# Last layer's MLP for two of three token groups: the inner product in seven block products instead of eight

## The chip, the cores and the metric

The kernel runs on one core of one Trainium2 chip. The metric is the device time of one execution in microseconds. Lower is better.

A core has a matrix engine (TensorE, PE in the profile), which writes its results into eight PSUM banks, three engines for elementwise work (VectorE or DVE, ScalarE or ACT, GpSimd or POOL), and queues that issue DMAs (here mostly that of SyncE, SP).

## The reference, cut to what matters

Two layers of a decoder, 1040 prompt tokens (16 of them learned) and 8 sample tokens, all in float32. Layer 0 has a convolution module, layer 1 a recurrent one (RWKV-7), and each is followed by an MLP:

```python
h = h + out                                   # out: the mixer's, through w_o in layer 1
h = h + jnp.square(jax.nn.relu(_rmsnorm(h, norm_mlp[i]) @ w_mlp_in[i])) @ w_mlp_out[i]
...
y = _rmsnorm(h, norm_final)
```

The width is D = 1024, the hidden width of the MLP DFF = 4096. In this text the product with w_mlp_in is the inner one, the product with w_mlp_out the outer one.

## The kernel before, in words

**Layout.** Activations lie transposed: 128 features on the partitions, KT = 8 blocks of features, tokens along the free dimension. A matmul takes a 128x128 block of weights as stationary operand and up to 352 tokens as moving operand. The last layer's tokens come in three groups G2: group 0 with 328 tokens, groups 1 and 2 with 352 each.

**Precision.** A float32 product is made of three matmuls in the faster format F32R: each operand is split into a high part (a cast, on ACT) and a low part (the difference, on DVE or POOL), and `mm3` (L188) multiplies high by high, low weight by high activation, and high weight by low activation.

**Weights.** `load_raw` (L144) brings 512 KB by a DMA on SP into one of five buffers. `load_w` (L150) casts them to high parts on ACT (L158, 128x1024 at once) and makes the low parts on POOL in four operations of 128x256 (L165). Five such pairs of buffers (`open_weights`, tag w) let ACT and POOL run ahead of PE.

**The last stage** (from L1621): for group 0 the mixer's output projection (`mixer_out`, L1637: for 8 blocks m, `dense` with 24 matmuls each, then h += result on DVE and the squares for the norm), then its MLP alone, with the rest of the recurrent mixer filled in between. Then the projections of groups 1 and 2, and one MLP for both, so that each weight block serves both groups. `final` (L1662) applies the last norm, transposes and writes out.

**The MLP** (`mlp`, L322). The normalised activations are not scaled by 1/rms: `mlp_in` (L273) multiplies h by the norm's weights only, splits, and 1/rms is multiplied in when the inner result leaves PSUM (L347: max(x, 0) times 1/rms on DVE; L348: square on ACT; L141 and L142: high and low part). `inp` does one of 32 column blocks j for one group: 8 blocks k of three matmuls into one bank. `out` does the outer product: for two rows of weights (j, j+1) and each of the 8 output blocks m, six matmuls into a bank, which DVE adds to h (L360). So each pair of column blocks has 2 x 2 x 24 = 96 inner and 2 x 8 x 6 = 96 outer matmuls. There are 16 such pairs.

**What sets the order.** Inside `in_order()` PE's instructions stand in program order; the other engines' order is set by a list scheduler, which takes what is ready by its own model of time, the earliest in the program first. All engine queues are in order on the chip. `filler` spreads the steps of other work over the points of the main loop. Before, `final(0)` is spread over group 2's projection and the MLP, and group 1's `final` over the last outer products of group 2.

**PSUM**: four banks "mm" for products, one "x" for means, three "w" for transposes.

Of the kernel before, what the change touches and what calls it, by code (L numbers as in the profile page):

```python
# [8 lines left out]
F32 = mybir.dt.float32  # L9
F32R = mybir.dt.float32r  # L10
# [36 lines left out]
def hybrid_step(tc, x_prompt, x_sample, state_conv, state_shift, state_wkv, meta_tokens,  # L47
# [10 lines left out]
    with ctx:  # L58
# [129 lines left out]
        def mm3(ps, w, act, first, last):  # L188

            nc.tensor.matmul(ps, w[0], act[0], start=first, stop=False)  # L190
            nc.tensor.matmul(ps, w[1], act[0], start=False, stop=False)  # L191
            nc.tensor.matmul(ps, w[0], act[1], start=False, stop=last)  # L192
# [4 lines left out]
        def dense(w, act, n, name, fill=None):  # L197
            ps = bank(f"ps_{name}")
            for k in range(KT):
                mm3(ps[:, :n], (w[0][:, k, :], w[1][:, k, :]), [tile_of(part, k)[:, :n] for part in act], k == 0, k == KT - 1)  # L200
                if fill and k == KT // 2 - 1:
                    fill()
            return ps

# [572 lines left out]
        hsum = masks.tile([P, P], F32, name="hsum")  # L777
        nc.vector.memset(hsum, 0.0)
        for sl in HALF:
            nc.vector.memset(hsum[sl, sl], 1.0)  # L780
        cur["raw"] = pool(lm, "wrawd", 5)
        cur["mm"] = pool(lm, "psum1", 4, space=PSUM)
        cur["x"] = pool(lm, "psx1", 1, space=PSUM)
        cur["w"] = pool(lm, "psw", 3, space=PSUM)
# [7 lines left out]
        hsel = masks.tile([P, 4 * KT + 2 * (KT - 1)], F32, name="hsel")  # L792
        nc.vector.memset(hsel, 0.0)
        for q in range(2):
            for e in range(2):
                o = 2 * (KT - 1) + NH * e + q
                nc.vector.memset(hsel[HALF[q], o:o + 1], 1.0)
        head_sel = lambda p: hsel[:, 2 * (KT - 1 - p):2 * (KT - 1 - p) + 2 * NH]
# [9 lines left out]

        hspread = masks.tile([P, NH, HS], F32R, name="hspread")
        nc.vector.tensor_copy(hspread, r_head.unsqueeze(2).broadcast_to([P, NH, HS]))  # L810
# [20 lines left out]
        lorap = pool(ld, "lorap", 1)  # L831
        pr = pool(ld, "pr", 1)
# [15 lines left out]
        sps = masks.tile([P, KT, DEC], F32, name="sps")  # L848
# [772 lines left out]
        with ExitStack() as l1:  # L1621
            open_tmp(l1, N2, "2", 3, False)
            open_weights(l1, 0, {"w": 5}, "f")
# [3 lines left out]
            hidp = pool(l1, "hidp1", 2)  # L1627
            hl = {}
# [8 lines left out]
            def mixer_out(g, actp, fill, add):  # L1637
                lo, n = G2[g]
                h1 = hl[g]
                block = lambda m: load_col(rwkv_w_o[0], m, f"wo{g}_{m}", nc.gpsimd, keep=m > 0)  # L1640
# [21 lines left out]
            def final(g):  # L1662
                lo, n = G2[g]
                hv = hl[g][:, :, :n]
                accs = mean_parts(hv, n, f"f{g}", True, "facc")
# [21 lines left out]
                for j, i in enumerate(starts):  # L1687
# [3 lines left out]
                    ot = (outp if g < 2 else cur["raw"]).tile([P, D], F32, name=f"ot{g}_{i}", tag="raw")  # L1691
                    for hf in range(2):
                        pt = bank(f"pf{g}{i}{hf}", "w" if g < 2 or hf else "mm")
# [54 lines left out]
            outp = pool(l1, "outp", 1)  # L1748
# [10 lines left out]
            end = []  # L1759

            def done(g):
                end.append(filler(KT, ([final(g)], 24)))

            def fill2():
                (end[0][0] if end else fill)()
            mlp(1, [g1, group(2, actp2, hidp2, sums)], 1, nc.gpsimd, nc.vector, fill2, done)
            for it in (rest, end[0][1], final(2)):
                for _ in it:
                    pass
# [31 lines left out]
```

## Time and profile before

| | |
|---|---|
| median of 3 runs | 2635.03 us (2635.01 to 2638.54) |
| span of the profiled execution | 2635.4 us |
| PE busy | 2581.3 us, 98%, 19956 matmuls |
| DVE, ACT, POOL busy | 1707.6, 1139.1, 1457.0 us |
| projections of groups 1 and 2 | about 2054 to 2117 us |
| MLP of groups 1 and 2 | about 2117 to 2622 us |
| last `final` alone | about 2622 to 2635 us |

The span goes from the first to the last instruction of the one profiled execution; for that execution no other time is shown, so the span is the time that the sums are made against, and it lies 0.4 us above the median of the runs. A line of the profile names the line of the code, the engine, the operation, output and inputs by tile names without numbers, their shapes, and how many there are; then the busy time, the mean duration of one in ns, and the idle time of the engine ahead of them with what ended it. For PE the durations overlap: a matmul's share of the time is read from the distance of the starts, not from its duration.

### The profile page before, as it was taken

The page shows a single profiled execution, that of the slowest core. Times are in us where ns is not written, and L with a number is a line of the kernel's source. Part 1 is how long each engine was busy: PE and PEld are TensorE (multiplying, and loading weights), DVE is VectorE, ACT ScalarE, POOL GpSimd, SP SyncE. Part 2 cuts the span into 40 slices and gives each one's busy share as a digit, 9 for nine tenths or more (in the row PEclk, how much of TensorE's full clock was granted, in tenths as well). Part 3 has the DMA queues.
Part 4 walks back from the last instruction along what each step waited for, and adds up shares of the span by engine and source line. Part 5 has one row for each costly group of instructions (what it writes and reads, how often), then busy time and mean ns, then how long its engine had stood idle before and what let it go on. Part 6 is the DMA issues. An engine that isn't in the chain of part 4 may idle for free.

```text
span 2635.4 us, 51726 instructions
## 1 busy us (share of the span) xinstructions
PE 2581.3 (98%) x19956; PEld 2436.7 (92%) x19956; DVE 1707.6 (65%) x3587; ACT 1139.1 (43%) x2110; POOL 1457.0 (55%) x2066
## 2 busy tenths in 40 slices
PE   8999999999999999999999999899999999999998
PEld 8999999999999999877788877799999999999998
DVE  6999999997544344544857567686689543444435
ACT  5546445444534333233345545555444542222223
POOL 7677878878878877122111213476588763333331
PEclk9999999999999999999999999999999999999999
DMA  6663544554446543668876967898575542222211
GB/s 190 173 168 108 164 142 133 160 169 139 137 144 174 163 142 113 184 201 210 225 192 191 226 158 190 234 195 197 152 213 175 138 133 71 66 73 65 73 49 45
DMA packets 602061, 400.24 MB, mean 152 GB/s; under 512 B 96128, under 2 KB 548928, under 8 KB 601814
## 3 DMA queue, kind: packets, MB, share of 16 engines
q1 hardware_dynamic: 573764, 360.08, 49.6%
q0 software_dynamic: 8720, 26.35, 3.3%
q10 hardware_dynamic: 19330, 10.49, 1.4%
q8 instruction: 158, 2.59, 0.4%
q14 instruction: 89, 0.73, 0.1%
HBM read 338.94 MB, written 58.83 MB: 151 GB/s over the span
## 4 chain that ended last, share of the span: by engine, by line
PE 84%; DVE 9%; DMA 2%; ACT 2%; issue 2%; POOL 1%; ACTq 0%; SPq 0%; DVEq 0%; POOLq 0%
PE ps_in L190 8%; PE ps_in L192 8%; PE ps_in L191 8%; PE out L190 8%; PE out L191 8%; PE out L192 8%; PE pk L922 4%; PE pr L922 4%; PE pv L922 3%; PE ps_o L192 1%; PE ps_o L190 1%; PE ps_o L191 1%; PE ps_g L190 1%; PE ps_g L191 1%; PE ps_g L192 1%
## 5 line engine op out<-in xcount | busy, mean ns | idle before, releaser
L165 POOL TENSOR_TENSOR wo_lo<-wo_raw,wo_hi 128x256 fp32r<-128x256 f32 x736 | 543.2, 770 | 285.1 <-ACT wo_hi L158 282.6
L165 POOL TENSOR_TENSOR wi_lo<-wi_raw,wi_hi 128x256 fp32r<-128x256 f32 x640 | 473.4, 772 | 237.3 <-ACT wi_hi L158 236.7
L190 PE MATMUL out<-hh,wo_hi 128*128 128x352 f32 (+2 forms) x1536 | 497.4, 324 | 9.2 <-DVE h L360 7.6
L360 DVE TENSOR_TENSOR h<-h,out 128x352 f32<-128x352 f32 (+2 forms) x768 | 386.6, 511 | 168.8 <-PE out L192 167.0
L190 PE MATMUL ps_in<-m_h,wi_hi 128*128 128x352 f32 (+2 forms) x1536 | 493.9, 322 | 0.0
L192 PE MATMUL ps_in<-m_l,wi_hi 128*128 128x352 f32 (+2 forms) x1536 | 492.8, 321 | 0.7 <-DVE m_l L288 0.7
L191 PE MATMUL out<-hh,wo_lo 128*128 128x352 f32 (+2 forms) x1536 | 492.5, 321 | 0.0
L191 PE MATMUL ps_in<-m_h,wi_lo 128*128 128x352 f32 (+2 forms) x1536 | 491.4, 320 | 0.0
L192 PE MATMUL out<-hl,wo_hi 128*128 128x352 f32 (+2 forms) x1536 | 490.8, 320 | 0.0
L542 DVE SCALAR_TENSOR_TENSOR cv<-u,wdw,cv 128x348 f32<-128x348 f32 (+2 forms) x720 | 378.1, 575 | 0.7
L158 ACT CAST wi_hi<-wi_raw 128x1024 fp32r<-128x1024 f32 x160 | 167.7, 1050 | 383.3 <-PE out L192 190.9
L158 ACT CAST wo_hi<-wo_raw 128x1024 fp32r<-128x1024 f32 x184 | 192.8, 1049 | 312.4 <-PE out L192 167.5
L190 PEld LDWEIGHTS out<-hh,wo_hi 128*128 128x128 f32 x1536 | 289.1, 188 | 15.0 <-DVE h L360 10.4
L190 PEld LDWEIGHTS ps_in<-m_h,wi_hi 128*128 128x128 f32 x1536 | 289.2, 188 | 1.5
L192 PEld LDWEIGHTS ps_in<-m_l,wi_hi 128*128 128x128 f32 x1536 | 288.2, 188 | 2.0 <-DVE m_l L288 1.5
L191 PEld LDWEIGHTS out<-hh,wo_lo 128*128 128x128 f32 x1536 | 288.5, 188 | 0.8
L191 PEld LDWEIGHTS ps_in<-m_h,wi_lo 128*128 128x128 f32 x1536 | 288.5, 188 | 0.6
L192 PEld LDWEIGHTS out<-hl,wo_hi 128*128 128x128 f32 x1536 | 288.2, 188 | 0.0
L347 DVE SCALAR_TENSOR_TENSOR ps_in<-ps_in,rs_m 128x352 f32<-128x352 f32 (+2 forms) x192 | 100.6, 525 | 259.2 <-PE ps_in L192 258.8
L142 DVE TENSOR_TENSOR hl<-ps_in,hh 128x352 fp32r<-128x352 f32 (+2 forms) x192 | 98.8, 515 | 124.9 <-ACT hh L141 124.8
L348 ACT ACTIVATE ps_in<-ps_in 128x352 f32<-128x352 f32 (+2 forms) x192 | 85.1, 444 | 130.0 <-DVE ps_in L347 129.8
L1099 POOL DMA_DIRECT2D d_n<-n x32 | 24.5, 764 | 185.8 <-DVE n L1089 93.4
(371 smaller groups left out, 4727.6 us busy)
## 6 DMA issues: line engine op xcount, KB each, us to landing
wi_raw<-in_w_mlp_in_dram SPq DMA_DIRECT2D x160, 512.0 KB
wo_raw<-in_w_mlp_out_dram SPq DMA_DIRECT2D x160, 512.0 KB
wk_raw<-in_rwkv_w_k_dram SPq DMA_DIRECT2D x32, 512.0 KB
wr_raw<-in_rwkv_w_r_dram SPq DMA_DIRECT2D x32, 512.0 KB
wv_raw<-in_rwkv_w_v_dram SPq DMA_DIRECT2D x32, 512.0 KB
d_ab<-ab POOLq DMA_DIRECT2D x32, 512.0 KB, 4.6
pg_raw<-in_conv_w_pw_dram SPq DMA_DIRECT2D x24, 512.0 KB
pa_raw<-in_conv_w_pw_dram SPq DMA_DIRECT2D x24, 512.0 KB
```

Source lines behind the costliest of these rows:

```text
L142: return eng_lo.tensor_sub(lo, src, hi.bitcast(F32))
L158: cast = nc.scalar.copy(hi[:, :a * b], raw[:, :a * b])
L165: eng_lo.tensor_sub(lo[:, cs], raw[:, cs], hi[:, cs].bitcast(F32))
L190: nc.tensor.matmul(ps, w[0], act[0], start=first, stop=False)
L191: nc.tensor.matmul(ps, w[1], act[0], start=False, stop=False)
L192: nc.tensor.matmul(ps, w[0], act[1], start=False, stop=last)
L347: nc.vector.scalar_tensor_tensor(s, s, 0.0, rs()[:, :n], op0=ALU.max, op1=ALU.mult)
L348: nc.scalar.activation(s, s, AF.Square)
L360: total = nc.vector.tensor_add(hv[:, 4 * i + m, :], hv[:, 4 * i + m, :], ps[:, :n])
L542: nc.vector.scalar_tensor_tensor(acc[m][:, :n], ug[:, m, j:j + n], wdw[:, m, j:j + 1], acc[m][:, :n], op0=ALU.mult, op1=ALU.add)
L922: nc.tensor.matmul(ps[:, :n], w[:, k, :], act[k], start=k == 0, stop=k == KT - 1)
L1099: nc.gpsimd.dma_start(d_n[ch0:ch0 + ncg, p].rearrange("c r t -> r c t"), n32[:, :ncg])
```

## The change

**The product.** For groups 1 and 2 the inner product is taken as a product of 2x2 blocks. The activations are halved by features (four blocks k each) and by group, the weights by the same features and by two column blocks 2s, 2s+1. Four result blocks from eight block products become seven block products of sums and differences of blocks (Winograd's form of Strassen's scheme). Each is four blocks k of three matmuls. There are 16 steps s.

- The activations are now scaled by 1/rms first (`normed`), then differences are formed and split: `later_half` does group 1's part during group 2's projection, `first_half` group 2's part after the first product.
- The weights' sums and differences are four DVE operations of 128x512 per step (`weight`). `unit` replaces `load_w` for groups 1 and 2: half a block (128x512), one cast on ACT and two subtractions on POOL, in eight pairs of buffers.
- The results' sums are formed partly in PSUM (a product is added onto a bank that holds another one, once that one has been copied out by ACT or read by DVE), partly by DVE additions on eviction. Then come max and square in one DVE operation, then the split.
- A hand-written order: the first two steps' products together in the order 7, 3, 7, 3, 1, 2, 1, 2, 6, 6, 4, 4, 5, 5; then per step "1762543" with the outer products of the step before in between.

**Moved.** `final(0)` goes into group 1's projection, its output tiles into the five load buffers. At the end the last outer products of group 2 come first, with five of them ahead of product 3; then those of group 1 with `final(2)` between them; then `final(1)`. PSUM from the projections on: three banks "mm", one "x", two "V", one "Z", one "X". The weight buffers of group 0's MLP are closed before the half-block buffers open. Four small constants (hsum, hsel, hspread, sps) go to a pool that is closed earlier.

```diff
+        def unit(src, name, keep=False):
+            hi, lo = (cur["units"].tile([P, UK, P], F32R, name=f"{name}_{q}", tag="u" + q, bufs=UB) for q in "hl")
+            a, b = src.shape[1:]
+            hv, lv = (t.rearrange("p k c -> p (k c)").rearrange("p (a b) -> p a b", a=a) for t in (hi, lo))
+            cast = nc.scalar.copy(hv, src)
...
+            step = 2 * P // b
+            for i in range(0, a, step):
+                nc.gpsimd.tensor_sub(lv[:, i:i + step], src[:, i:i + step], hv[:, i:i + step].bitcast(F32))
...
+            lf.close()
             cur["wide"] = wide
+            cur["units"] = pool(l1, "units", UB)
+            mixed_w = pool(l1, "mixw", 5)
...
+            fill, rest = filler(2 * KT, ([final(0)], FB))
             add, sums = sums_of(1)
             with in_order():
-                mixer_out(1, actp, lambda: None, add)
-            g1 = group(1, actp, hidp, sums)
-            fill, rest = filler(2 * KT + MLP2_POINTS, ([ranked(FN, final(0))], FB))
+                mixer_out(1, actp, fill, add)
...
+            def later_half(sums):
+                norm1 = normed(1, sums)
...
+                for k in range(UK):
+                    yield 1
+                    norm1(k)
+                    norm1(UK + k)
+                    t3 = tt(f"t3_{k}", "t1")[:, :n]
+                    nc.vector.tensor_sub(t3, f32_of[1][UK + k], f32_of[1][k])
+                    parted("7", k, t3, nc.vector)
+                    yield 1
+                    parted("3", k, f32_of[1][UK + k], nc.vector)
...
+            lps.close()
+            for tag, bufs in (("mm", 3), ("x", 1), ("V", 2), ("Z", 1), ("X", 1)):
+                cur[tag] = pool(l1, f"pair{tag}", bufs, space=PSUM)
...
+            def first_half(sums):
+                norm2 = normed(2, sums)
...
+                a, b = f32_of[1], f32_of[2]
+                for i in range(2):
+                    for k in range(UK):
+                        norm2(i * UK + k)
+                        parted("12"[i], k, b[i * UK + k], nc.vector)
+                for k in range(UK):
+                    nc.vector.tensor_sub(a[k], a[k], b[k])
+                    nc.vector.tensor_sub(a[UK + k], a[UK + k], a[k])
+                    parted("6", k, a[UK + k], nc.vector)
+                for k in range(UK):
+                    nc.vector.tensor_sub(b[UK + k], b[UK + k], a[UK + k])
+                    parted("4", k, b[UK + k], nc.gpsimd)
+                for k in range(UK):
+                    parted("5", k, a[k], nc.gpsimd)
...
+                    nc.vector.tensor_add(s1, a21, a22)
+                    nc.vector.tensor_sub(a21, a11, a21)
+                    nc.vector.tensor_sub(s2, s1, a11)
+                    nc.vector.tensor_sub(s4, a12, s2)
+                    sums_w[s] = {"1": a11, "2": a12, "3": s4, "4": a22, "5": s1, "6": s2, "7": a21}
...
+            def product(s, q, early=False):
+                w = weight(s, q)
+                tag = "Y" if early and q == "3" else {"2": "X", "7": "Z", "4": "Z"}.get(q, "V")
+                first = tag == "Y" or q in "127"
+                if first:
+                    held[s, tag] = bank(f"{tag}{s}", "mm" if tag == "Y" or early and s and tag == "Z" else tag)[:, :n]
+                ps = held[s, tag]
+                for k in range(UK):
+                    mm3(ps, block_of([w], k), [t[k][:, :n] for t in hi_lo[q]], first and k == 0, k == UK - 1, not first)
...
+            ORDER, LAST = "1762543", "1276453"
+            MID, END = (0, 2, 3, 3, 3, 3, 2), (0, 0, 2, 4, 5, 5, 0)
+            with in_order():
+                product(0, "7", True)
+                first_half(sums)
+                product(0, "3", True)
+                for q in "73":
+                    product(1, q, True)
+                for s in range(2):
+                    for q in "12":
+                        product(s, q, True)
+                for q in "645":
+                    for s in range(2):
+                        product(s, q)
+                pend = outs(0)
+                take(pend, 2 * KT)
...
-            mlp(1, [g1, group(2, actp2, hidp2, sums)], 1, nc.gpsimd, nc.vector, fill2, done)
```

More of the change, by code (lines that the diff above doesn't have):

```diff
@@ L186, in col_stream, with mm3 @@
                 yield blocks_of(raws.pop(i))
[L188 to L192, printed above, removed]
+        def mm3(ps, w, act, first, last, onto=False):
+            nc.tensor.matmul(ps, w[0], act[0], start=first, stop=False, skip_group_check=onto)
+            nc.tensor.matmul(ps, w[1], act[0], start=False, stop=False, skip_group_check=onto)
+            nc.tensor.matmul(ps, w[0], act[1], start=False, stop=last, skip_group_check=onto)
+        UK, UB = KT // 2, 8
         def bank(name, tag="mm"):
@@ L831, in hybrid_step @@
         lorap = pool(ld, "lorap", 1)
+        hsum = lorap.tile([P, P], F32, name="hsum")
+        nc.vector.memset(hsum, 0.0)
+        for sl in HALF:
+            nc.vector.memset(hsum[sl, sl], 1.0)
+        hsel = lorap.tile([P, 4 * KT + 2 * (KT - 1)], F32, name="hsel")
+        nc.vector.memset(hsel, 0.0)
+        for q in range(2):
+            for e in range(2):
+                o = 2 * (KT - 1) + NH * e + q
+                nc.vector.memset(hsel[HALF[q], o:o + 1], 1.0)
+        head_sel = lambda p: hsel[:, 2 * (KT - 1 - p):2 * (KT - 1 - p) + 2 * NH]
+        hspread = lorap.tile([P, NH, HS], F32R, name="hspread")
+        nc.vector.tensor_copy(hspread, r_head.unsqueeze(2).broadcast_to([P, NH, HS]))
         pr = pool(ld, "pr", 1)
@@ new lines, in first_half @@
+            def first_half(sums):
+                norm2 = normed(2, sums)
+                acts = new_acts(actp2, "b1", wide)
+                hi_lo["1"], hi_lo["2"] = ([t[i * UK:(i + 1) * UK] for t in acts] for i in range(2))
+                six = residp.tile([P, KT, wide], F32R, name="t2", tag="h")
+                hi_lo["6"] = [[six[:, i * UK + k, :] for k in range(UK)] for i in range(2)]
+                spare = [("ey", 3), ("eq", 1), ("ebv", 1), ("egt", 2)]
+                five = [wn.tile([P, KT * HS], F32R, name=f"t1_{tag}{i}", tag=tag, bufs=b)[:, :n] for tag, b in spare for i in range(b)]
+                five += [combp.tile([P, wide], F32R, name="t1_7")]
+                four = [combp.tile([P, wide], F32R, name=f"t4_{i}") for i in range(KT)]
+                hi_lo["5"], hi_lo["4"] = ([t[:UK], t[UK:]] for t in (five, four))
+                a, b = f32_of[1], f32_of[2]
[12 more added lines that the diff above has]
+                    parted("5", k, a[k], nc.gpsimd)
@@ new lines, in evict, with squared, snap @@
+            def evict(s, i, g, c):
+                if (g, s) not in hid:
+                    hid[g, s] = [HID[g].tile([P, 2, wide], F32R, name=f"h{q}1{g}_{s}", tag=f"h{q}") for q in "hl"]
+                hh, hl_ = hid[g, s]
+                split(hh[:, i, :n], hl_[:, i, :n], c, nc.vector)
+            def squared(c):
+                nc.vector.scalar_tensor_tensor(c, c, 0.0, c, op0=ALU.max, op1=ALU.mult)
+            def snap(name, ps, tag=None, bufs=1):
+                t = (stat(name, tag, bufs) if tag else tt(name, "t2"))[:, :n]
+                nc.scalar.copy(t, ps)
+                return t
@@ new lines, in out_weight, with out @@
+            def out_weight(s, u):
+                if (s, u // 2) not in raws:
+                    src = w_out[2 * s * P:(2 * s + 2) * P, u * 2 * P:(u + 2) * 2 * P].rearrange("(j p) c -> p j c", p=P)
+                    raws[s, u // 2] = load_raw(src, (2, 4 * P), f"wo1_{s}_{u // 2}").rearrange("p (a b) -> p a b", a=2)
+                return unit(raws[s, u // 2][:, :, u % 2 * 2 * P:(u % 2 + 1) * 2 * P], f"wo1_{s}_{u}")
+            def out(s, m, g, w):
+                hh, hl_ = hid[g, s]
+                ps = bank(f"out1_{s}_{g}_{m}")
+                for j in range(2):
+                    c = slice(m % 2 * P, (m % 2 + 1) * P)
+                    mm3(ps[:, :n], [part[:, j, c] for part in w], (hh[:, j, :n], hl_[:, j, :n]), j == 0, j == 1)
+                nc.vector.tensor_add(hl[g][:, m, :n], hl[g][:, m, :n], ps[:, :n])
@@ new lines, in outs, with take @@
+            def outs(s):
+                for u in range(KT // 2):
+                    w = out_weight(s, u)
+                    for g in G:
+                        for m in (2 * u, 2 * u + 1):
+                            out(s, m, g, w)
+                            yield
+            def take(it, count):
+                for _ in range(count):
+                    next(it, None)
+            ORDER, LAST = "1762543", "1276453"
+            MID, END = (0, 2, 3, 3, 3, 3, 2), (0, 0, 2, 4, 5, 5, 0)
@@ new lines, in hybrid_step @@
+            with in_order():
+                product(0, "7", True)
[11 more added lines that the diff above has]
+                take(pend, 2 * KT)
+                pend = outs(1)
+                for s in range(2, NS - 1):
+                    for q, o in zip(ORDER, MID):
+                        product(s, q)
+                        take(pend, o)
+                    take(pend, 2 * KT)
+                    pend = outs(s)
+                s = NS - 1
+                ws = []
+                for q, o in zip(LAST, END):
+                    if q == "3":
+                        take(pend, 2 * KT)
+                        ws = [out_weight(s, u) for u in range(KT // 2)]
+                        for m in range(5):
+                            out(s, m, G[0], ws[m // 2])
+                    product(s, q)
+                    take(pend, o)
+                for m in range(5, KT):
+                    out(s, m, G[0], ws[m // 2])
+                fill, rest = filler(KT, ([final(G[0], "mm")], 24))
+                for m in range(KT):
+                    out(s, m, G[1], ws[m // 2])
+                    fill()
@@ L1768, in hybrid_step @@
+            for it in (rest, final(G[1], "V")):
                 for _ in it:
```

110 lines of the change are left out of this document (79 added, 31 removed).

## The prediction, made before the result was known

> **What bounds the kernel now.** I read the page's busy table and slices first, then the windows of the last 600 us, the groups of the steady stretch, the waits of PE, and last the groups and instructions around the two places where the change adds work.
>
> ```profile
> PE 2581.3 (98%) x19956; PEld 2436.7 (92%) x19956; DVE 1707.6 (65%) x3587; ACT 1139.1 (43%) x2110; POOL 1457.0 (55%) x2066
> PEclk9999999999999999999999999999999999999999
> ```
>
> TensorE is busy 98% of the span at full granted clock. In the windows (columns: busy time and instructions of PE, PEld, DVE, ACT, POOL, granted clock, DMA share, GB/s):
>
> ```profile
> 2054.00:2085.00 31.00, 31.00 (x199) 30.52 (x198) 17.38 (x35) 20.39 (x41) 23.32 (x28) 1.00 0.45 121
> 2085.00:2117.00 32.00, 31.68 (x195) 30.54 (x195) 14.58 (x19) 15.20 (x24) 23.53 (x30) 1.00 0.45 129
> ...
> 2200.00:2300.00 100.00, 100.00 (x626) 100.00 (x625) 39.56 (x76) 25.63 (x42) 36.75 (x52) 1.00 0.23 69
> ```
>
> The first two rows are the two output projections of groups 1 and 2, the third a stretch of their MLP: PE never idle, DVE at 40%, POOL at 37%. PE's waits from 1900 us to the end are these, the first two before 2042 us:
>
> ```profile
> PE out L190 <- DVE h L360: 5.0, 5, 1.4
> PE out L190 <- DVE hl L142: 1.3, 2, 0.9
> PE ps_oo L191 <- POOL wo_lo L165: 0.3, 1, 0.3
> ```
>
> DVE was full there, 19.73 of 20 us:
>
> ```profile
> 1960.00:1980.00 20.00, 18.37 (x120) 17.79 (x119) 19.73 (x45) 7.64 (x12) 16.93 (x21) 1.00 0.62 178
> ```
>
> So in the changed stage there is no stall to win; only fewer matmuls can help, and every microsecond that PE newly waits is lost in full. The groups of the MLP from 2170 to 2560 us (count | busy us, mean ns | idle before):
>
> ```profile
> L190 PE MATMUL ps_in<-m_h,wi_hi 128*128 128x352 f32 x404 | 130.2, 322 | 0.0
> L360 DVE TENSOR_TENSOR h<-h,out 128x352 f32<-128x352 f32 x203 | 105.9, 521 | 83.8 <-PE out L192 83.7
> L165 POOL TENSOR_TENSOR wo_lo<-wo_raw,wo_hi 128x256 fp32r<-128x256 f32 x104 | 73.7, 741 | 126.1 <-ACT wo_hi L158 126.1
> L142 DVE TENSOR_TENSOR hl<-ps_in,hh 128x352 fp32r<-128x352 f32 x52 | 27.2, 523 | 44.6 <-ACT hh L141 44.6
> L347 DVE SCALAR_TENSOR_TENSOR ps_in<-ps_in,rs_m 128x352 f32<-128x352 f32 x51 | 27.2, 533 | 103.8 <-PE ps_in L192 103.8
> L141 ACT CAST hh<-ps_in 128x352 fp32r<-128x352 f32 x51 | 23.1, 454 | 1.6
> ```
>
> The 322 ns of a matmul overlaps its neighbours; the spacing is 100 us over 626 = 0.160 us. The 51 casts of L141 bear that out: one per 24 inner and 24 outer matmuls, 390/51/48 = 0.159 us.
>
> The Trainium skill (TensorE: Matmul & The Clock Gate, "Back-to-back issue gap") gives N/2.4 + 2.5 ns, which is 149 ns at 352 columns. The trace has 160 ns; by the page the removed matmuls would weigh 28.6 us rather than the 30.7 below, and the measurement decides.
>
> **The matmuls removed.** The reach is 16 steps s. One step held 2 blocks x 2 groups x 8 k x 3 = 96 inner matmuls and holds 7 x 4 x 3 = 84 after it; the 96 outer ones stay. 16 x 12 = 192 matmuls of the same shape and spacing go: 192 x 0.160 = **30.7 us**. Transposes, the mean matmuls (st_m) and the projections keep their counts.
>
> **Work added per steady step** (31 us before, 28.8 after). Four sums of 128x512 weights on DVE, which this trace shows alone and beside a busy POOL as
>
> ```profile
> L1187 DVE TENSOR_TENSOR ab<-rk,ex 128x512 f32<-128x512 f32 x32 | 22.8, 713 | 0.0
> L1539 DVE TENSOR_TENSOR egt<-ebv,egt 128x512 f32<-128x512 f32 x6 | 5.6, 940 | 0.1
> ```
>
> make 2.9 to 3.8 us. Seven half-blocks are cast and split where there were four: six more POOL subtractions, 4.4 us (22 x 0.74 = 16 of 28.8). Three bank copies on ACT cost 3 x 0.45. Evictions have three additions from a bank (0.52), three squarings and four low parts with both inputs in SBUF (0.5 to 0.95). DVE comes to 16 x 0.52 + 3.3 + 1.6 + 7 x 0.7 = 18 of 28.8 us, ACT to about 11. PE covers all of it on average. What can fail is order: a product that adds onto a bank (6 onto 1, 5 and 3 after it, 4 onto 7) waits for the ACT copy or DVE addition of it, and everything in PE's hand-written order stands behind it. Between such pairs lie at least 24 matmuls, 3.8 us, against about 1 us of copy and queue. The outer matmuls now rotate over three banks instead of four. Cost: 0 to 6 us over all steps, taken as **2**, nearer the clean row than the stalls of 2042 us, which came with DVE full.
>
> **The start of the pair** is the real price. Before, the activations went in unscaled (the 1/rms was applied at eviction, L347), so PE had work at once. Now norms of both groups, their differences and high and low parts must exist first. Before, this place showed:
>
> ```profile
> L288 DVE SCALAR_TENSOR_TENSOR m_l<-h,pvec,m_h 128x352 fp32r<-128x352 f32 x8 | 7.2, 947 | 0.6 <-ACT m_h L287 0.5
> L142 DVE TENSOR_TENSOR z_l<-zr,z_h 128x352 fp32r<-128x352 f32 x8 | 5.0, 663 | 4.7 <-ACT z_h L141 4.7
> L165 POOL TENSOR_TENSOR wo_lo<-wo_raw,wo_hi 128x256 fp32r<-128x256 f32 x52 | 41.7, 836 | 12.6 <-ACT wo_hi L158 11.1 <-issue 1.5
> L263 POOL TENSOR_TENSOR acc_m<-sq,sq 128x352 f32<-128x352 f32 x2 | 1.9, 952 | 2.1 <-ACT sq L252 2.1
> L268 ACT ACTIVATE sd_m<-st_m,eps_t 128x352 f32<-128x352 f32 x1 | 0.5, 548 | 0.0
> ...
> 2117.08 1.35 PE L241 MATMUL st_m<-acc_m,ones_d 128*128 128x352 f32 x4
> ...
> 2131.65 2.35 DVE L270 RECIPROCAL rs_m<-sd_m 128x352 f32<-128x352 f32 x1 [0.88 <-ACT sd_m L268]
> ```
>
> A DVE operation on 352 columns with both inputs in SBUF takes 0.52 us alone (as L142 above, one input in PSUM) and 0.66 to 0.95 beside POOL. During group 2's projection DVE gets 20 such operations of group 1, after a mean that stands 36 matmuls (5.8 us) into it; I let 3 us (0 to 5) spill past its end, and count the time from there. Product 7 ends at 1.9 + 3; st_m takes 1.35, the root 0.55, the reciprocal 2.35: with the semaphores between them the norm of group 2 begins at 9.3 us, while PE has products 3, 7, 3 to work (to 12). DVE then runs 32 operations: 8 until product 1 is fed, 16 for 2, 28 for 6, 32 for 4, with some 3 of an eviction among them. At 0.7 us each (between the two rows, since POOL halts once its eight half-blocks are full) the last is done at 9.3 + 35 x 0.7 = 33.8, with cast and POOL's subtraction (about 1.5) 35.3; products 4, 4, 5, 5 then run to about 41.5. Without waits PE would need 14 x 12 x 0.160 + 1.35 = 28.2. Stall: **13 us**. At 0.52 and no spill it is about 4, at 0.95 about 22. The eviction backlog (24 operations) runs under the 96 outer matmuls of step 0, 15.4 us, which is just its length.
>
> **Smaller edits.** The half-blocks of group 1's projection lie where the last weights of group 0's MLP lay, so their first cast (about 0.65, an estimate from L141's 0.454 at 352 columns) and two subtractions (2 x 0.84) may wait for PE's last use: 0 to 6 us, taken as **1.5**, since only the first buffer meets a late one. final(0) moves from the MLP into this projection: six squared sums, eight scalings, six evictions beside 11 to 14 us that ACT and DVE have free there; its output DMAs stand on SP ahead of later weight loads, and its tiles come out of the five load buffers, but the load behind the first of them has some 12 us to spare: 0 to 2, nothing taken. In the tail, the final of the first group to finish now has 48 matmuls (7.7 us) as cover where it had 72; the last part stays:
>
> ```profile
> 2624.86 0.54 DVE acc_f L233
> 2625.40 0.04 issue
> 2625.44 1.18 PE fs L1679 x10
> ```
>
> from the last addition to the end is 10.5 us either way. −1 to 4, taken as **1.5**. hsum, hsel, hspread and sps change their pool only: nothing, 1 us if they wait.
>
> **Sum.** −30.7 + 2 + 13 + 1.5 + 1.5 = −12.7 us. The profiled span is 2635.4 and the median of the runs 2635.03, so nothing measurable lies around the span: 2635.0 − 12.7 = **2622 us**. With all low ends −30.7 + 4 − 1 = −28, with all high ones −30.7 + 22 + 6 + 6 + 4 + 3 = +10.
>
> **The rivals.**
>
> *The start is short* (stalls of 10 us or less in all): DVE at 0.52 because POOL worked ahead; the 12.6 us that POOL idled in the projections speak for it, 20 more DVE operations in them against it. 2605 to 2614 us.
>
> *DVE and POOL take turns.* If no operation of DVE with two SBUF inputs ran beside one of POOL, the stretch from the first projection to the last early product would hold, at quiet durations, POOL's 92 x 0.741 and 17 of 352 columns at about 0.95 = 84 us, and DVE's 85 x 0.52 + 8 x 0.713 = 50 us. 134 us, less some 12 us worked ahead, against PE's 96 (2 x 30.7 + 28.2, and some 6 of means and transposes): 26 us of stall. With the other terms −30.7 + 26 + 5 = 0: 2635 us. For it: the same shapes stretch beside POOL, 0.52 to 0.95 and 0.74 to 0.84. Against it: in the L288 row both engines were near full and neither doubled. The Trainium skill (SBUF — State Buffer, "SBUF: two separate sides") calls the port pair of the two engines an exclusive lock held for the full instruction; the stretching agrees in direction, and its full form is this rival.
>
> *The weight sums hold up the outer additions: slower.* With three banks, an outer result must be added before the bank's next turn: three outer tiles of 0.96 us and a product of 1.92 give 3.84 us, less the addition 3.3. Four sums in a row on DVE's in-order queue take 2.9 alone, 3.8 beside POOL, and 4 x (0.713 + 0.741) = 5.8 if each first waits out one of POOL's. From 3.3 us on PE stops; at 5.8 it is 2.5 us in each of 14 steps, 35 us: 2622 + 33 = 2655 us. Against: DVE has 10 us free per step, and the raw weights come early enough to spread the sums.
>
> *The saving isn't there.* The loop counts leave no room: 84 matmuls a step for 96; no chance of its own.
>
> **How the numbers follow.** Forecast 0.60, short start 0.18, taking turns 0.14, weight sums 0.08. A measurement of this kernel tells about 0.2% (5.3 us) from no change. Faster needs less than 25 us of stalls: all of the short start, nearly all of the forecast, hardly any of the others: 0.76. Within 0.2%: 0.16, the turns and the forecast's worst end. Slower: 0.08. The range 2608 to 2638 leaves out the best third of the short start and the weight sums; the forecast's own is 2612 to 2633.
>
> **What would show it.** Right: 192 matmuls fewer, 0.160 us spacing in the middle of the pair with no PE idle time, a steady step of 28.8 us, and PE waits of 9 to 17 us in the 60 us after group 2's projection, released by DVE (norms, differences) and POOL (low parts of 4 and 5). Wrong: PE waits in every step behind h additions (weight sums), a start without waits, PE waiting in the projections for POOL (turns), or a spacing other than 0.160.

## The result, and the profile after

The changed kernel takes 2666.7 us (median, 2664.08 to 2671.18), the kernel before on the same chip 2636.07 us (2635.01 to 2638.54). The ratio is 1.0117, with an interval of 1.0103 to 1.0131: slower by some 30 us, where 2622 us had been forecast.

The page of the changed kernel, busy time and granted clock; its span is 2662.3 us, 26.9 us more than before:

```profile
PE 2571.5 (97%) x19764; PEld 2422.5 (91%) x19764; DVE 1820.4 (68%) x3723; ACT 1187.7 (45%) x2264; POOL 1589.1 (60%) x2170
PEclk9999999999999999999999999899999999999999
```

The matmuls are 192 fewer, as forecast, but PE is idle for 90.8 us of the span instead of 54.1, and the clock row has one slice below 9. The same stretch of the steady steps in both traces, before first, then after (PE busy, then DVE, ACT and POOL, as in the windows above):

```profile
2250.00:2550.00 300.00, 300.00 (x1873) 300.00 (x1873) 120.16 (x232) 74.46 (x118) 110.20 (x156) 1.00 0.23 69
```

```profile
2250.00:2550.00 300.00, 300.00 (x1856) 300.00 (x1855) 178.28 (x308) 107.21 (x205) 198.97 (x229) 1.00 0.26 74
```

Neither has any idle time here, so the steady steps work as forecast: 180 matmuls in 29.1 us for 192 in 30.8. The loss lies elsewhere. The times at which PE passes four places (first or last matmul of a stage, by its start, and the end of the span):

| us | before | after | difference of the stage |
|---|---|---|---|
| group 1's projection begins | 2054.0 | 2068.2 | +14.2 |
| group 2's projection ends | 2121.8 | 2146.3 | +10.3 |
| last outer product | 2621.6 | 2649.8 | +3.7 |
| end of the span | 2635.4 | 2662.3 | -1.3 |

The 2117 us given above as the end of the projections before is the first matmul of the MLP; the last one of the projection is at 2121.8.

More than half of the loss has happened before group 1's projection begins. It falls into group 0's projection (ps_oo with the recurrence's filled-in steps): 53.1 us before, 66.6 after. PE's longest waits there, 1695 to 1772 us (total, count, longest), before and after:

```profile
PE A L1287 <- DVE fs L1405: 2.6, 2, 2.4
```

```profile
PE A L1308 <- DVE fs L1426: 12.1, 2, 7.7
```

A and fs belong to the recurrence, which no line of the block products touches. From 2060 us on, PE waits in the changed kernel for these:

```profile
PE V L192 <- DVE b_l L142: 8.8, 2, 7.7
PE out L192 <- DVE hl L142: 4.3, 2, 3.5
PE st_m L262 <- ACT sq L273: 3.4, 1, 3.4
PE fs L1706 <- POOL acc_f L254: 3.0, 1, 3.0
```

The first three belong to the start of the pair (0.8 us of the second to the last step), the fourth is final(0) in group 1's projection. No row has a wait in each step.

### The profile page after: what moved, and what is told of

Its sections match the earlier page's. It is cut to its first block, busy times and chain, and to the rows that moved or that the text cites. A ratio compares the mean times of both kernels' runs of the same rounds, so it can differ in the third digit from the quotient of the medians.

```text
span 2662.3 us, 51898 instructions
## 1 busy us (share of the span) xinstructions
PE 2571.5 (97%) x19764; PEld 2422.5 (91%) x19764; DVE 1820.4 (68%) x3723; ACT 1187.7 (45%) x2264; POOL 1589.1 (60%) x2170
## 4 chain that ended last, share of the span: by engine, by line
PE 80%; DVE 11%; DMA 3%; POOL 2%; ACT 2%; issue 2%; ACTq 0%; SPq 0%; DVEq 0%; POOLq 0%
PE out L190 8%; PE out L192 8%; PE out L191 8%; PE ps_in L190 5%; PE ps_in L191 5%; PE ps_in L192 5%; PE pk L943 4%; PE pr L943 4%; PE pv L943 3%; PE V L192 1%; PE V L190 1%; PE V L191 1%; PE ps_o L192 1%; PE ps_o L190 1%; PE ps_o L191 1%
## 5 line engine op out<-in xcount | busy, mean ns | idle before, releaser
L190 PE MATMUL out<-hh,wo_hi 128*128 128x348 f32 (+2 forms) x1024 | 332.3, 324 | 8.8 <-DVE h L381 7.4
L190 PE MATMUL ps_in<-m_h,wi_hi 128*128 128x348 f32 (+2 forms) x1024 | 328.7, 321 | 0.0
L192 PE MATMUL ps_in<-m_l,wi_hi 128*128 128x348 f32 (+2 forms) x1024 | 327.2, 320 | 0.5 <-DVE m_l L309 0.5
L191 PE MATMUL ps_in<-m_h,wi_lo 128*128 128x348 f32 (+2 forms) x1024 | 326.8, 319 | 0.0
L191 PE MATMUL out<-hh,wo_lo 128*128 128x348 f32 (+2 forms) x1024 | 326.7, 319 | 0.0
L192 PE MATMUL out<-hl,wo_hi 128*128 128x348 f32 (+2 forms) x1024 | 326.6, 319 | 0.0
L381 DVE TENSOR_TENSOR h<-h,out 128x348 f32<-128x348 f32 (+2 forms) x512 | 253.3, 505 | 69.5 <-PE out L192 67.8
L223 POOL TENSOR_TENSOR wo_l<-wo_raw,wo_h 128x256 fp32r<-128x256 f32 x192 | 163.7, 877 | 73.1 <-ACT wo_h L218 69.0
L192 PE MATMUL out<-hl,wo_h 128*128 128x352 f32 x512 | 167.3, 327 | 4.3 <-DVE hl L142 4.3
L190 PE MATMUL out<-hh,wo_h 128*128 128x352 f32 x512 | 167.6, 327 | 0.2 <-ACT hh L141 0.2
```

What stands on the lines that cost most here:

```text
L190: nc.tensor.matmul(ps, w[0], act[0], start=first, stop=False, skip_group_check=onto)
L191: nc.tensor.matmul(ps, w[1], act[0], start=False, stop=False, skip_group_check=onto)
L192: nc.tensor.matmul(ps, w[0], act[1], start=False, stop=last, skip_group_check=onto)
L223: nc.gpsimd.tensor_sub(lv[:, i:i + step], src[:, i:i + step], hv[:, i:i + step].bitcast(F32))
L381: total = nc.vector.tensor_add(hv[:, 4 * i + m, :], hv[:, 4 * i + m, :], ps[:, :n])
```

## The experiments

Runs made together share one chip and its runs of the kernel before (medians of 2636.7, 2638.3, 2638.6 and 2637.1 us in the four lots), so kernels of different lots are compared by their ratios to it; 0.001 is 2.6 us.

### The buffers

Two theories for the 14.2 us: the places of the buffers, or something that the block products set off early. The kernel before, with one or both of the moves and nothing else of the change:

```diff
-            open_weights(l1, 0, {"w": 5}, "f")       # e1_both, e1_wpool
...
             hidp = pool(l1, "hidp1", 2)
+            open_weights(l1, 0, {"w": 5}, "f")
...
-        hsum = masks.tile([P, P], F32, name="hsum")  # e1_both, e1_consts; hsel, hspread and sps alike
...
+        hsum = lorap.tile([P, P], F32, name="hsum")
```

> The kernel before with the two moves of buffers alone: the four constants go into the pool that closes earlier, and the weight buffers of group 0's MLP are opened after the activations' pools. No block products. In the changed kernel group 1's projection began 14.2 us later than before (2068.2 against 2054.0 us of the span), before any block product. Theory (the moves cause it): the same lateness here, 2649 us, with the waits of the recurrence's matmuls (A for fs) at 1715 to 1757 us. Rival (the scheduler changed its order there because of the new stage behind it): 2635 us, group 1's projection at 2054 us.

> The kernel before with the place of group 0's MLP weight buffers alone moved. If this move makes the lateness, group 1's projection begins at about 2068 us and the span is about 2649 us; if the constants make it, 2054 and 2635 us.

> The kernel before with the four constant tiles in lorap, as in the change, and the weight pool of group 0's MLP where it was. Theory 1, each move costs by itself: both together cost 27.5 us and the weight pool alone 15.7, so this one costs the other 12: 2648 us. Theory 2, the constants' move costs only together with the weight pool's: 2636 to 2639 us.

Both: 2664.17 us, ratio 1.0103 (1.0086 to 1.0120). That is nearly the whole loss of the change without one block product, and twice what was expected. The weight pool alone: 2652.44 us, in one run only. The constants alone: 2642.29 us, ratio 1.0014 (1.0004 to 1.0025), 4 us and neither of the two numbers expected. As far as one run tells, the moves do not simply add.

The other way round, the change with its buffers where they were. To fit there, its block weights take seven pairs of half-block buffers instead of eight and its weight sums six instead of five:

```diff
+            cells = [cur["wsp"].tile([P, 8 * P], F32R if i < 7 else F32, name=f"cell{i}", tag="w" + "hl"[i % 2], bufs=5) for i in range(10)]
+            halves = [c[:, i * UK * P:(i + 1) * UK * P] for c in cells[7:] for i in range(2)]
...
-            hi, lo = (cur["units"].tile([P, UK, P], F32R, name=f"{name}_{q}", tag="u" + q, bufs=UB) for q in "hl")
+            hi, lo = cur["units"]()                  # the next of cells[:7], high and low half
...
+                dead = hspread.rearrange("p h c -> p (h c)")
+                four = [dead[:, i * n:(i + 1) * n] for i in range(2)] + [combp.tile([P, wide], F32R, name=f"t4_{i}") for i in range(2, KT)]
```

> The changed kernel with its seven block products, but with the weight pool of group 0's MLP and the four constant tiles opened where the kernel before opens them. To fit, the block weights and block sums are kept in that weight pool's ten buffers (seven units and six sums instead of eight and five), and two of T4's tiles in hspread, which nothing reads by then. Theory 1, the two moves cost 27.5 us by where they put the buffers: 2640 us, group 0's projection back from 66.7 to 53 us, spacing in the steady pair steps back from 0.1618 to about 0.1605 us. Theory 2, the moves' cost and the block products' are not separable (in the changed kernel the order on the queues is set by something else): 2655 us or more, group 0's projection over 62 us.

2636.79 us, ratio 0.9998 (0.9986 to 1.0010): theory 1. Group 0's projection takes 52.1 us, and the steady stretch is this (1870 matmuls, 0.1604 us apart):

```profile
2250.00:2550.00 300.00, 300.00 (x1870) 300.00 (x1869) 182.51 (x311) 109.59 (x211) 198.64 (x230) 1.00 0.25 74
```

So the moves cost the 30 us, and the block products by themselves are worth nothing, where 12 us had been forecast: two errors to explain. The profiled executions of the change and of f1_places lie 27.8 us apart: 14.6 in group 0's projection, 5.5 in those of groups 1 and 2, 6.8 from there to the last outer product (3.7 of it in the start of the pair), 0.9 elsewhere.

### How a move of buffers costs time

In the kernel before, by the addresses that the allocator gave, the first weight buffers of group 0's projection lie on tiles that group 3's mixing was done with (hx, mx); in the change most of them lie on tiles read at the very end of group 3 (st, rk, vv). The first cast comes later, at 1690.8 us before and 1700.4 after (the second at 1702.2 and 1701.4), and the order in SP's queue turns round. SP's issues (start, duration), before and after:

```profile
1696.59 0.37 SPq L147 DMA_DIRECT2D wo_raw<-in_rwkv_w_o_dram  x1
1703.60 0.33 SPq L1235 DMA_DIRECT2D ni<-d_n  x1
...
1705.87 8.37 SPq L147 DMA_DIRECT2D wo_raw<-in_rwkv_w_o_dram  x4
```

```profile
1695.88 7.88 SPq L147 DMA_DIRECT2D wo_raw<-in_rwkv_w_o_dram  x3
1707.47 0.34 SPq L1256 DMA_DIRECT2D ni<-d_n  x1
```

Before, the loads that wait for buffers stand behind ni, the recurrence's input; after, in front of it. Yet it is not the place in the queue that holds ni: SP's queue is idle from 1703.8 us on after, and ni is issued 0.3 us after the landing of d_n, which it reads, in both kernels (landings at 1703.3 and 1707.2 us). The write of d_n is the slower one. From issue to landing it takes, before and after:

```profile
DMA to landing us min/median/max: 3.1/3.1/3.1
```

```profile
DMA to landing us min/median/max: 5.7/5.7/5.7
```

Meanwhile the DMA engines move 260 GB/s before and 325 after. DVE then waits for ni, its first operation on it starts at 1711.1 us instead of 1707.1, and fs comes later:

```profile
1711.12 0.21 DVE L1270 TENSOR_TENSOR tt<-ni 128x30 f32<-128x30 f32 x1 [9.62 <-DMA ni<-d_n]
```

The second of the two waits of A is of another kind. DVE and POOL of the changed kernel:

```profile
1746.87 9.63 DVE L284 TENSOR_TENSOR acc_m<-acc_m,sq 128x328 f32<-128x328 f32 x1 [1.79 <-ACT sq L273]
1756.43 0.68 DVE L1426 TENSOR_TENSOR fs<-S,wc 128x512 f32<-128x512 f32 x1
```

```profile
1745.17 2.80 POOL L165 TENSOR_TENSOR wo_lo<-wo_raw,wo_hi 128x256 fp32r<-128x256 f32 x4
1747.94 8.20 POOL L165 TENSOR_TENSOR wi_lo<-wi_raw,wi_hi 128x256 fp32r<-128x256 f32 x12
```

One addition of 328 columns takes 9.63 us (0.69 in the kernel before), until POOL's run of late subtractions ends, and fs stands behind it on DVE's queue. Two kernels, each from e1_both, take one of the two away:

```diff
-            nc.sync.dma_start(ni, blocks(d_n))                      # h1_ni
+            st["ni"] = nc.sync.dma_start(ni, blocks(d_n)).ins
...
+                    with nullcontext() if g or not m else tc.issue_after(st["ni"]):
+                        raw = load_raw(src, (KT, P), f"wo{g}_{m}")
```

```diff
+            quiet = name in ("wi1_0_0", "wi1_0_1", "wi1_0_2")       # h2_quiet
+            if quiet:
+                nc.scalar.copy(lo[:, :a * b], raw[:, :a * b])
-            for c in range(0, a * b, step):
+            for c in range(0, 0 if quiet else a * b, step):
```

> The kernel before with both moves of buffers, with one thing changed on SP's queue: group 0's output-weight loads 1 to 7 (wo_raw) are issued after the recurrence's load of ni, not three of them ahead of it. Theory 1, the first wait of A for fs in group 0's projection (7.6 us) comes from ni standing behind loads that wait for buffers: ni goes from 1710.5 to about 1703 us, the wait to under 3 us, total 2655 to 2659 us. Theory 2, the weights' own lateness (first cast 1702.5 instead of 1690.8 us) is what the recurrence waits on, through POOL and ACT: no gain, 2662 us or more.

> The kernel before with both moves of buffers; the low parts of the first three input weights of group 0's MLP are made as ACT copies of the value instead of POOL differences, so those parts of the output are not the reference's. Takes twelve back-to-back operations (8.2 us) off POOL beside which one DVE sum took 9.65 us. Theory 1, that long DVE operation makes the second wait of A for fs (7.2 us): the operation back to about 1 us, the wait under 2 us, total 2656 to 2659 us. Theory 2, the recurrence is late there anyhow: total 2662 us or more.

h1_ni: ratio 1.0084 (1.0063 to 1.0104) against 1.0103 (1.0086 to 1.0120) of e1_both, 5 us less, which these intervals do not tell from nothing. d_n lands 2.3 us after its issue (6.6 in e1_both; 125 GB/s meanwhile against 298), ni is issued at 1702.97 us, and of e1_both's two waits (14.7 us) these are left, of which the second, with an acc_m of 8.51 us ahead of it, is the 5.9 (the first went from 7.6 to 2.1, and a wait of 2.8 us for nr came in):

```profile
PE A L1287 <- DVE fs L1405: 8.0, 2, 5.9
```

h2_quiet: ratio 1.0056 (1.0036 to 1.0077), 12 us less, clear of the noise and more than expected. The addition and PE's waits:

```profile
1750.17 0.50 DVE L266 TENSOR_TENSOR acc_m<-acc_m,sq 128x328 f32<-128x328 f32 x1
```

```profile
PE A L1290 <- DVE fs L1408: 4.7, 1, 4.7
```

Theory 1 holds in h2_quiet. In h1_ni the time of ni and the wait are those of theory 1, but not its mechanism: the loads delay d_n, it seems by what they move beside it, and no run leaves their order and takes their bytes away. The first wait also differs among the kernels with the loads in front (4.4 us in the change, 7.6 in e1_both, 4.7 in h2_quiet), so how much of the total it costs is not shown. The contention of DVE and POOL weighs more. The Trainium skill (SBUF — State Buffer, "SBUF: two separate sides") has the loser of the port pair fully blocked for one instruction of the other engine. The trace goes further: POOL's operations took 0.68 us each (8.20 over 12), and DVE's was held over all of them.

A third part of the price is the spacing of matmuls. Before, e1_consts, e1_wpool and e1_both have the same instructions in their steady steps. Their counts in 2250 to 2550 us are 1873, 1864, 1861 and 1845, with PE busy throughout and the clock at 1.00; the last of them:

```profile
2250.00:2550.00 300.00, 300.00 (x1845) 300.00 (x1844) 118.19 (x228) 74.99 (x119) 109.27 (x155) 1.00 0.23 67
```

300/1873 = 0.1602 us and 300/1845 = 0.1626: over the pair's 3072 matmuls 7.4 us. From group 2's projection to the last outer product e1_both takes 507.0 us, before 499.8. With h1's 5 and h2's 12 that would be about 24 of e1_both's 27 us, if the three add and h1's gain is real; they were not taken away together. What in the addresses changes the spacing stays open.

### Why the block products gain nothing

At the old places the start of the pair runs from 2125.4 us to the first steady product at 2193.0: 67.6 us for 263 matmuls of 0.1604 and 8 mean matmuls, 44.9 us of work. So 22.7 us are lost, where 13 were forecast. PE's waits of f1_places, 2050 to 2640 us:

```profile
PE V L192 <- DVE b_l L142: 7.8, 2, 6.7
PE out L192 <- DVE hl L142: 4.4, 2, 3.5
PE X L190 <- DVE c L1925: 2.7, 1, 2.7
```

Waits at the start sum to 15.4 us (6.67, 3.51, 2.75, 1.10, 0.78, 0.57). The other 7.3 us lie in matmuls that ran slower. Right behind the longest wait the matmuls follow each other at 0.29 to 0.30 us:

```profile
2143.74 0.66 PE L192 MATMUL V<-b_l,cell 128*128 128x352 f32 x1 [6.67 <-DVE b_l L142]
2144.20 0.49 PE L190 MATMUL V<-b_h,cell 128*128 128x352 f32 x1
2144.50 0.49 PE L191 MATMUL V<-b_h,cell 128*128 128x352 f32 x1
```

```profile
2143.00:2150.00 7.00, 5.16 (x15) 4.33 (x16) 7.00 (x11) 1.97 (x6) 3.85 (x5) 0.50 0.23 67
```

The granted clock is 0.50 for these 7 us. By the Trainium skill (TensorE: Matmul & The Clock Gate, "Part 1: The HAM clock gate") an idle window of about 3.4 us brings the clock to one half; the trace agrees, with 6.67 us idle and full spacing back at 2150.7 us. Two more stretches of 3.4 us at half clock begin at 2157.5 and 2178.0 us, right behind or in the waits of 2.75 and 3.51 us; the first of these waits is shorter than that window. In the first stretch no time is idle:

```profile
2157.40:2161.00 3.60, 3.60 (x15) 3.60 (x14) 1.59 (x2) 0.00 (x0) 3.60 (x5) 0.53 0.41 146
```

What holds the start: DVE's amount of work, POOL's beside it, their order, or the chain through group 2's mean? Six kernels. Three start from the changed kernel as it was:

```diff
+                def low(q, k, src):                                 # e3_order: DVE's order by hand, low part two steps behind
+                    hi, lo = (t[k] for t in hi_lo[q])
+                    nc.scalar.copy(hi, src)
+                    late.append(lambda: nc.vector.tensor_sub(lo, src, hi.bitcast(F32)))
+                    if len(late) > 2:
+                        late.pop(0)()
```

> The changed kernel with DVE's work at the start of the pair in a written order: each low part two operations behind its norm or difference, where the scheduler had put eight norms and three differences ahead of the first low part. Theory 1 (the order is what makes TensorE wait): the wait of 7.7 us for the first low part goes and with it the halved clock behind it, 8 to 11 us in all. Theory 2 (DVE's amount of work is what binds): product 1 starts earlier, but products 2 and 6 wait instead, and no more than 4 us are won.

2670.78 us, ratio 1.0130 (1.0113 to 1.0146): no gain. The one wait of 7.69 us became four of 0.66 to 2.19 us, and the start is as long (72.8 us for 71.2). The order of DVE's work is not the cause.

```diff
+            if quiet:                                               # e6_quiet: s < 2
+                nc.scalar.copy(lv, src)
```

> The changed kernel with the low parts of the first two steps' inner weights left out: ACT copies the weights in their place, so that POOL's 28 subtractions of them go. Theory (DVE and POOL hold each other up at the start): DVE's operations of 352 columns fall from 0.97 to 0.52 us there, and the stretch from the first block product to step 2 falls from 71 us by 8 to 13. Rival (DVE's own work and the chain of the norm bind): 71 us stays within 3.

Ratio 1.0102 (1.0087 to 1.0117): the start is some 3 us shorter (68.3 us).

```diff
-                        parted("12"[i], k, b[i * UK + k], nc.vector) # e5_lows; T6's alike
+                        both("12"[i], k, b[i * UK + k])             # nc.scalar.copy into high and low
```

> The changed kernel with the twelve low parts of T1, T2 and T6 made as second ACT copies of the value instead of DVE differences (the products then use the value twice, so the output is not the reference's). Takes twelve operations off DVE at the start of the pair and puts twelve on ACT. Theory 1, the amount of DVE's work sets the start: 8 to 10 us less of the start (71 to about 62 us), total about 2658 us. Theory 2, the chain through reciprocal, norms and differences sets it, and the lowered clock behind every wait: at most 3 us less, about 2664 us.

Ratio 1.0094 (1.0074 to 1.0114): some 3 us of the start (68.1 us). Neither engine's share alone is the cause, and the chain through the norm was left as the suspect. That was put to the test at the old places, with group 2 normalised by group 1's factor:

```diff
+                if g == 1:                                          # f2_norm
+                    hi_lo["rs"] = rstd_of(mean_bcast(sums, n, f"m1{g}"), n, 0, f"m1{g}", "rsm", 2)
+                rs = hi_lo["rs"]
```

> The changed kernel with the buffers at their places of before (2636.8 us), with group 2 normalised by group 1's factor, so that nothing at the start of the pair waits for group 2's mean square, its root and its reciprocal (the output is not the reference's). Theory 1, the 192 matmuls saved are given back at the start of the pair, where the norm has to come before the sums of blocks: the start, 67.6 us with 45 us of matmuls in it, shrinks by 12 to 20 us and the total falls to 2617 to 2625 us. Theory 2, the amount of DVE's and POOL's work at the start holds it whenever it begins: less than 6 us.

Ratio 1.0003 (0.9991 to 1.0014) against 0.9998: nothing. The steady steps begin at 2196.1 us, not earlier, and the start is 67.4 us, though no V waits for a norm any more. Group 2's operations now come before the early products' weights and low parts, and those are late:

```profile
PE Y L190 <- ACT cell L218: 5.2, 2, 3.7
PE Y L191 <- POOL cell L223: 4.3, 2, 3.1
PE Z L192 <- DVE b_l L142: 2.8, 1, 2.8
```

So the chain's wait alone is not it, though DVE's order changed with it, and both amounts at once were taken away, with and without the norm's wait (the edits of e5_lows and e6_quiet together on f1_places, then with that of f2_norm):

> The changed kernel with the buffers at their places of before (2636.8 us) and less work at the start of the pair: the twelve low parts of T1, T2 and T6 are ACT copies of the value, not DVE differences, and the low parts of the first two steps' inner weights are ACT copies, not POOL differences (the output is not the reference's). Each of the two, alone in the changed kernel, took some 3 us off. Theory 1, DVE and POOL hold each other up at the start, so that the amount on both sets it: both together take 10 to 15 us off, total 2622 to 2627 us. Theory 2, the chain of mean square, root, reciprocal, norm and sum sets it, whatever lies beside it: the two add up to 6 us or less, total 2630 us or more.

> The same with less work at the start, and group 2 normalised by group 1's factor, so that the wait for group 2's mean square is gone too (the output is not the reference's). Theory 1, the amount sets the start: no more than 4 us below the kernel with less work alone. Theory 2, the chain sets it: 8 to 14 us below that kernel.

i1_less: ratio 0.9960 (0.9941 to 0.9979), 10 us below f1_places. i2_less_norm: 0.9975 (0.9965 to 0.9986), nothing more. Theory 1's number holds at its low end: the start shrinks from 67.6 to 58.5 us. In the changed kernel the two amounts taken singly gave some 6 us together, so this gain alone does not show that the engines hold each other up; the durations do. The same eight norms on DVE, in f1_places and in i1_less:

```profile
2134.03 6.65 DVE L1809 SCALAR_TENSOR_TENSOR nf<-h,pvec,rs_m 128x352 f32<-128x352 f32 x8
```

```profile
2136.15 4.06 DVE L1811 SCALAR_TENSOR_TENSOR nf<-h,pvec,rs_m 128x352 f32<-128x352 f32 x8
```

0.83 us each beside POOL's low parts, 0.51 without them. The lock works the other way too: in f1_places two POOL subtractions stand still while DVE runs its sums back to back from 2148 to 2156 us:

```profile
2149.98 7.12 POOL L223 TENSOR_TENSOR cell<-wi_raw,cell 128x256 fp32r<-128x256 f32 x2 [3.15 <-ACT cell L218]
```

In i1_less the start still loses some 13.6 us, with waits for c (2.6 us) and for the hidden's parts (2.5 and 0.6) among them; these were not taken apart further.

### Smaller parts, and a better version

```diff
-            fill, rest = filler(2 * KT, ([final(0)], FB))
+            fill, rest = filler(2 * KT, ([late_start(8), final(0)], FB))
```

> The changed kernel with final(0) beginning eight fill points later in group 1's projection. Theory 1, fs waits 3.0 us there because POOL's sum of squares is started just before: 3 to 5 us less, about 2663 us. Theory 2, final(0)'s 4.6 us of PE work and its DVE and ACT operations only come at another place of the same stage: no change, 2666 us.

Ratio 1.0082 (1.0061 to 1.0102) against 1.0117 (1.0103 to 1.0131) of the change. The projections take 72.6 us instead of 78.1, and the wait of fs is gone: theory 1, a little more than expected, though 2.5 us of it are lost again in the start, 73.7 us here. At the old places nothing is to be had there: f1_places has 72.6 us as it stands, 4.9 more than before; PE's share of final(0) in it is 3.6 us, where 1.2 stood before.

```diff
-                    held[s, tag] = bank(f"{tag}{s}", "mm" if tag == "Y" or early and s and tag == "Z" else tag)[:, :n]
+                    held[s, tag] = bank(f"{tag}{s}", "mm" if tag == "Y" or early and s and tag == "Z" else "x" if tag == "X" and s == 1 else tag)[:, :n]
...
                 pend = outs(0)
+                for q in "17":                                      # and left out of step 2's own turn
+                    product(2, q)
                 take(pend, 2 * KT)
```

> The changed kernel with the buffers at their places of before, and two more edits at the start of the pair: step 1's X product gets a bank of its own (the idle one of the sums), and products 1 and 7 of step 2 stand ahead of step 0's outer products, as cover for their 3.5 us wait for the hidden's low part. Theory 1, waits of X for c (2.75 us) and of the outer products for hl (0.8 and 3.5 us), and the lowered clock behind them, go: 2628 to 2632 us, faster than before by 0.2 to 0.4%. Theory 2, the two products only move the wait, since DVE works through the hidden's evictions at the same pace: 2634 to 2637 us.

> The changed kernel with the buffers at their places of before and the cover of two products of step 2 (2633.9 us), with DVE's order at the start written out by hand: each norm with its low part two steps behind it, instead of the norms first. Theory 1, the first low part comes 4 us earlier and the 5.7 us wait of the first block product for it goes: 2629 to 2631 us. Theory 2, as in the changed kernel with that order (no gain), the same waits come later in smaller pieces: 2633 to 2636 us.

g1_cover (f1_places with these lines): 2633.87 us, ratio 0.9989 (0.9979 to 0.9999), the fastest here of the kernels that leave nothing out, though by less than the 0.2% that the prediction called measurable and less than theory 1 had. The wait of X for c is gone, that of the outer products is 1.5 us instead of 4.3, and 2.4 us of waits for T6's low parts have come in. g2_order, the same with DVE's order by hand: ratio 1.0007 (0.9997 to 1.0017), no gain but some 5 us more; the waits of V come later and in smaller pieces, as in e3_order.

## Why the prediction was wrong

**"hsum, hsel, hspread and sps change their pool only: nothing, 1 us if they wait."** This is the step that failed. It priced the constants by their own waits and the weight pool of group 0's MLP not at all. Shown: both moves alone make the kernel before 27 us slower, and the change without them loses nothing. The prediction looked only at the stretch that the diff names; more than half of the price stands 350 us ahead of it, in group 0's projection, and the rest in the projections and in the spacing of the pair.

**The start of the pair, 13 us.** Right in its place and, for DVE, in its releasers; wrong in size: 22.7 us at the old places. POOL's low parts of 4 and 5 were waited for 1.6 us in the change and not at all at the old places. The norms begin 8.6 us after the projection, as forecast (9.3). Three things were missing. The clock after a long wait (7.3 us) was no term at all. The two engines held each other up more than "0.7 us each" allows (0.83 for the norms), and together the work taken away in i1_less is worth 9 us. And the "eviction backlog" does not run under the outer matmuls of step 0: these wait 4.3 us for its first pieces. The rival of DVE and POOL taking turns gave 26 us of stall and 2635 us, of all cases the nearest to f1_places. That nearness is in part luck: its mechanism shows in the norms and in POOL's 7.12 us, but it had no clock, and PE waits for POOL only 1.7 us, in group 2's projection.

**The matmuls removed, -30.7 us.** Right: 192 fewer, 0.1604 us apart at the old places.

**Steady steps, +2.** Right: 28.9 us in f1_places for 28.8 forecast, no PE idle; of the 2 us taken, 0.6 came, as spacing (0.1604 for 0.1602). In the change 29.1, by the places again (0.1616). The weight sums held up nothing; that rival is dead. (Its slack of 3.84 us is two outer tiles and a product; with the three that it names it would be 4.8.)

**Half-block buffers, +1.5; tail, +1.5.** The first is right in size, but f1_places waits its 2.1 us for weights in group 2's projection, not in group 1's. The tail is undersized: PE waits 4.3 us in the last step and the finals, where the kernel before waits 0.3.

**final(0), nothing.** Right at the old places. In the change it cost some 5 us of the projections, because POOL was behind there (e4_final).

At the old places the terms are -30.8 + 0.6 + 22.7 + 2.1 + 4.0 = -1.4 us; the span measured 0.9 us less than before, and the remaining 0.5 us was not taken apart. No rival on the slow side had to do with the places, so the 0.08 for "slower" went to a mechanism that did not occur.

## What to carry to other kernels

A pool that opens in another place is an edit of the schedule: ask which tiles lay there before, when their last reader is done, and what then runs beside what, transfers and engines alike, even hundreds of microseconds away. Keep the old places first, and measure the moves by themselves. A saving of matmuls that needs more elementwise work ahead of its first product has to be priced with that work's contention and with the clock that PE loses in the wait.

## What was not expected of the hardware

- One DVE addition that takes 0.50 us alone (h2_quiet) took 8.5 to 9.7 us in the kernels with the weight pool moved, beside a run of POOL subtractions with two SBUF inputs of 0.68 us each; two POOL subtractions took 7.12 us beside a run of such DVE operations.
- The spacing of the same matmuls, with no wait and at full clock, was 0.1602, 0.1609, 0.1612 and 0.1626 us in four kernels that differ only in where their buffers lie.
